# Four small edits around the attention and state-space stages of a two-layer encoder kernel

## The chip, the cores and the metric

The kernel runs on one core of one Trainium2 chip. The metric is the device time of one execution in microseconds (us).

## What is computed

The reference is a trunk of two layers on one sequence of 256 tokens of width 2048, all in float32. Cut to what matters here, a layer computes

```
h    = rms_norm(x)
proj = h @ w_in                    # cq 512 | ckv 256 + k_pe 64 | u 1024 | gates 2 x 2048
a    = mla(cq, ckv, k_pe)          # 16 heads: q, k of 128 + 64 (rope), v of 128
s    = s5(u)                       # 64 groups x 64 complex states, linear recurrence over time
m    = sigmoid(g_a) * a + sigmoid(g_b) * s
x    = x + rms_norm(m @ w_out)
x    = x + rms_norm(swiglu(rms_norm(x)) @ w_ffn_down)
```

Inside `mla`, a pair of heads at a time: `p = softmax(q k^T * scale)` with a block-causal mask, then `p @ v`. Inside `s5`: `bu = u @ B` (the input to each state), a recurrence along time, and `y = Re(C state) + D u`, then a gelu and a gated product with `w_glu`.

## The kernel before, in words

**Products.** Each float32 product is made of three products of float32r parts: a value is split into a high part (a copy that rounds) and a low part (value minus high part). Weights come from memory as tiles of 128x1024, one DMA on SP's queue each. ScalarE makes the high part `hi` (`Weights.high_to`, L179, its ACTIVATE at L187) and VectorE the low part `lo` (`split_to`, L191). `gemm` (L417) runs the three products at L448 to L450 for 16 row blocks of the weight; one `step` of it is six products on one half of the tokens. The products of an attention pair stand at L1387 to L1389 (q), L1414 to L1416 (k) and L1432 to L1434 (v).

**Order.** Instructions are emitted in an order written out by hand. `Background` (L74) is the planner. `later(d, fn)` puts a piece of work `d` steps ahead, `chain(d, fns)` puts several one step apart. `step(pe_ns)` (L118) adds one to the step count, emits what is due, and then emits pieces of the background generators as long as VectorE's planned time is less than `lead` ahead of TensorE's. Every VectorE instruction adds max(140, 75 + n/0.96) ns to VectorE's planned time, where n is the number of elements in a partition (`Counted`, L140, L150); ScalarE's instructions add nothing. All VectorE work goes through `Counted`, so it shows as L151 in the profile; ScalarE's goes through `act`, L268; a TensorE transpose is L494.

**S5.** `s5` (L915) is a background generator. It waits until its first state input is planned (`bu_due = bg.later(6, lambda: emit_bu(0))`, L1120), then runs 32 column tiles, each of which multiplies the tile's powers `E` with the state input `bu` (a tile `P` of 128x1024), adds, scans twice along time, multiplies again and adds to `xx`. `emit_bu` (L1069) is two TensorE products per tile, L1074; they read `us` and `bs`, stacked copies of u and of B that POOL fetches through memory (`load_stacks`, L1053, issues at L1063). After every four tiles `emit_y` (L1080) makes the output product, and a gelu of seven pieces writes `uz`. `prep_b` and `prep_c` transpose B and C into the bank `y`. The generator runs beside the input projections (stages u, ckv, cq, gates), the attention and the start of the product with `w_o`. `begin_glu` (L1466) empties the planner: it emits whatever of S5 is left, in the first product with `w_glu`, which reads `uz`, after six of its steps.

**Attention.** The loop over eight pairs (L1376) interleaves three pairs. At the top it makes the scores of the pair before (`scores`, L1311, products L1316 to L1319), and a step later come, one step each: the row maximum (VectorE), the exponentials (ScalarE), the reciprocal of the row sums (VectorE), the division (`norm`, L1339: four ScalarE ACTIVATEs, `p<-p,sts`). Below that stand q's rope part into the first half of `qp`, the product with v of two pairs before (`pv`, L1363; its output goes into `oT` in two parts, high on ScalarE two steps later and low on VectorE three steps later, shown as `H<-aux` and `H<-aux,H`), q's other two parts into `qn`, and the product that turns the rope part (L1401) into the second half of `qp`. A step later `rope` (L1219) reads it: `X<-X,rope`, `rtmp<-acc,rope`, `X<-X,rtmp`. Then k into `kk_ps`, the transposes of the divided exponentials (`trans_p`, L1347, shown as `aux<-cs,p`), and v into `v_ps`. ScalarE copies `qn`, `kk_ps` and `v_ps` out (`X<-acc` of 128x512).

`acc()` (L249) hands out one of three accumulator banks; a new tile waits until all readers of the bank's earlier tile are done. In the loop the four tiles `qp`, `qn`, `kk_ps`, `v_ps` of a pair share the three, so `v_ps` takes a bank of the same pair.

Of the kernel before, what the change touches and what calls it, by code (L numbers as in the profile page):

```python
# [13 lines left out]
AF = mybir.ActivationFunctionType  # L14
# [206 lines left out]
def trunk_kernel(ctx: ExitStack, tc: tile.TileContext, a: dict, out: bass.AP, cst: bass.AP,  # L221
# [27 lines left out]
    def acc():  # L249
        return T(pacc, [128, 512], "acc")  # L250
# [7 lines left out]
    def tsc(o, x, s1, op0, s2=None, op1=None):  # L258
        if op1 is None:
            V.tensor_scalar(out=o, in0=x, scalar1=s1, scalar2=None, op0=op0)  # L260
        else:
            V.tensor_scalar(out=o, in0=x, scalar1=s1, scalar2=s2, op0=op0, op1=op1)
# [4 lines left out]
    def act(o, x, f, **kw):  # L267
        ACT.activation(out=o, in_=x, func=f, **kw)  # L268
# [3 lines left out]
    def parts(hi, lo, src):  # L272
        return [lambda: act(hi, src, AF.Copy), lambda: tt(lo, src, hi.bitcast(F32), SUB)]
# [611 lines left out]
    for l in range(depth):  # L885
# [29 lines left out]
        def s5(l=l, gains=gains):  # L915
# [153 lines left out]
            def emit_bu(ct):  # L1069
                p, c = divmod(ct, 2)  # L1070
                bs, us = stacks[p]
                bu = T(ps5, [128, 2, S], "bu")
                for i in range(2):
                    PE.matmul(out=bu[:, i], lhsT=bs[:, c, 128 * i:128 * i + 128], rhs=us[:, c], start=True, stop=True)  # L1074
                bus[ct] = bu
                if c == 1:
                    used.append(p)
                    load_stacks()
# [38 lines left out]
            e_mirror(e)  # L1117
            while not stacks:
                yield
            bu_due = bg.later(6, lambda: emit_bu(0))  # L1120
            y_due = g_due = None
            xs = []
            yield
# [95 lines left out]
        def rope(dst, raw, rot):  # L1219
            tt(dst, raw, cosT, MUL)  # L1220
            tt(rtmp, rot, sinT, MUL)
            tt(dst, dst, rtmp, ADD)
# [88 lines left out]
        def scores(p, t):  # L1311
            sa, sb = aux(), aux()
            sa = sa.rearrange("p (h k) -> p h k", h=2)
            sb = sb[:, 0:256].rearrange("p (h k) -> p h k", h=2)
            for h_ in range(2):
                PE.matmul(out=sb[:, h_], lhsT=t["q"][:, h_, 0:128], rhs=t["k"][:, h_, 0:128], start=True, stop=False)  # L1316
                PE.matmul(out=sb[:, h_], lhsT=t["pe"][:, 0:128], rhs=kpeT[:, h_, 0:128], start=False, stop=True)
                PE.matmul(out=sa[:, h_], lhsT=t["q"][:, h_, 128:256], rhs=t["k"][:, h_], start=True, stop=False)
                PE.matmul(out=sa[:, h_], lhsT=t["pe"][:, 128:256], rhs=kpeT[:, h_], start=False, stop=True)  # L1319
            pr = T(ap, [128, 768], "p", bufs=2)  # L1320
            pb = pr[:, 0:256].rearrange("p (h k) -> p h k", h=2)
            pa = pr[:, 256:768].rearrange("p (h k) -> p h k", h=2)
            sts = T(vp, [128, 2, 4], "sts", bufs=2)

            def row_max():
                V.memset(ap=sb[0:64, :, 64:128], constant=NEG)
                V.memset(ap=sa[0:64, :, 192:256], constant=NEG)
                V.tensor_reduce(out=sts[:, 0, 0:2], in_=sb, axis=AX.X, op=ALU.max)
                V.tensor_reduce(out=sts[:, 0, 2:4], in_=sa, axis=AX.X, op=ALU.max)
                tsc(sts[:, 0], sts[:, 0], -SCALE, MUL)  # L1330

            def exps():
                for i, (s_, p_) in enumerate(((sb, pb), (sa, pa))):
                    for h_ in range(2):
                        j = 2 * i + h_
                        act(p_[:, h_], s_[:, h_], AF.Exp, scale=SCALE, bias=sts[:, 0, j:j + 1],
                            accum_out=sts[:, 1, j:j + 1])

            def norm():  # L1339
                for i, p_ in enumerate((pb, pa)):  # L1340
                    for h_ in range(2):
                        act(p_[:, h_], p_[:, h_], AF.Copy, scale=sts[:, 1, 2 * i + h_:2 * i + h_ + 1])

            bg.chain(1, [row_max, exps, lambda: V.reciprocal(out=sts[:, 1], in_=sts[:, 1]), norm])
            return pb, pa

        def trans_p(pp):  # L1347
# [15 lines left out]
        def pv(p, t, pT):  # L1363
            o = aux()
            for h_ in range(2):
                e = slice(128 * h_, 128 * h_ + 128)
                PE.matmul(out=o[:, 256 * h_:256 * h_ + 256], lhsT=t["v"][:, 0, e], rhs=pT[:, h_, 0:256],
                          start=True, stop=False)
                PE.matmul(out=o[:, 256 * h_ + 128:256 * h_ + 256], lhsT=t["v"][:, 1, e], rhs=pT[:, h_, 256:384],
                          start=False, stop=True)  # L1370
            bg.chain(2, parts(oT[:, 0, 2 * p:2 * p + 2], oT[:, 1, 2 * p:2 * p + 2],
                              o.rearrange("p (h t) -> p h t", h=2)))

        bg.lead = LEAD_ATT
# [1 line left out]
        for p in range(NPAIR):  # L1376
            t = par_tiles(p)
            if p >= 1:
                st_p[p - 1] = scores(p - 1, par_tiles(p - 1))
                bg.step(ATT * 2600)  # L1380
            base = W.pos
            qn, qp = None, acc()

            def proj(j, o):
                for k in range(4):
                    hi, lo = [t[:, k % 2, 128 * j:128 * j + 128] for t in W.get(base + k // 2, "q", base + 3)]
                    PE.matmul(out=o, lhsT=hi, rhs=cqT[:, 0, k], start=(k == 0), stop=False)  # L1387
                    PE.matmul(out=o, lhsT=lo, rhs=cqT[:, 0, k], start=False, stop=False)
                    PE.matmul(out=o, lhsT=hi, rhs=cqT[:, 1, k], start=False, stop=(k == 3))  # L1389

            proj(2, qp[:, 0:256])
            bg.step(ATT * 1300)
            bg.later(1, lambda t=t, qp=qp: act(t["raw"], qp[:, 0:256], AF.Copy))
            if p >= 2:
                pv(p - 2, par_tiles(p - 2), st_pT.pop(p - 2))
            bg.step(ATT * 1300)
            qn = acc()
            proj(0, qn[:, 0:256])
            bg.step(ATT * 1300)
            proj(1, qn[:, 256:512])  # L1400
            PE.matmul(out=qp[:, 256:512], lhsT=rperm, rhs=t["raw"], start=True, stop=True)  # L1401
            bg.later(1, lambda t=t, qp=qp: rope(t["pe"], t["raw"], qp[:, 256:512]))
            W.drop(base)
            W.drop(base + 1)
            bg.step(ATT * 1300)
            bg.later(1, lambda t=t, qn=qn: act(t["q"], qn.rearrange("p (h t) -> p h t", h=2), AF.Copy))
            base = W.pos
            hi, lo = W.get(base, "kv", base + 3)
            kk_ps = acc()
            for h_ in range(2):  # L1410
                o = kk_ps[:, 256 * h_:256 * h_ + 256]
                e = slice(256 * h_, 256 * h_ + 128)
                for k in range(2):
                    PE.matmul(out=o, lhsT=hi[:, k, e], rhs=ckvT[:, 0, k], start=(k == 0), stop=False)  # L1414
                    PE.matmul(out=o, lhsT=lo[:, k, e], rhs=ckvT[:, 0, k], start=False, stop=False)
                    PE.matmul(out=o, lhsT=hi[:, k, e], rhs=ckvT[:, 1, k], start=False, stop=(k == 1))  # L1416
            W.split_to(base + 1)
            bg.step(ATT * 1300)
            W.split_to(base + 2)
            bg.later(1, lambda t=t, kk_ps=kk_ps: act(t["k"], kk_ps.rearrange("p (h t) -> p h t", h=2), AF.Copy))  # L1420
            if p >= 1:
                st_pT[p - 1] = trans_p(st_p.pop(p - 1))
            bg.step(ATT * 650)
            v_ps = acc()
            hv = hi.rearrange("p k (h e) -> p k h e", h=2)[:, :, :, 128:256]
            lv = lo.rearrange("p k (h e) -> p k h e", h=2)[:, :, :, 128:256]
            for tb in range(NT):
                o = v_ps[:, 256 * tb:256 * tb + 256].rearrange("p (h e) -> p h e", h=2)
                for k in range(2):
                    xh = ckvT[:, 0, k, 128 * tb:128 * tb + 128]  # L1430
                    xl = ckvT[:, 1, k, 128 * tb:128 * tb + 128]
                    PE.matmul(out=o, lhsT=xh, rhs=hv[:, k], start=(k == 0), stop=False)  # L1432
                    PE.matmul(out=o, lhsT=xh, rhs=lv[:, k], start=False, stop=False)
                    PE.matmul(out=o, lhsT=xl, rhs=hv[:, k], start=False, stop=(k == 1))  # L1434
            W.drop(base)
            bg.later(1, lambda t=t, v_ps=v_ps: act(t["v"], v_ps.rearrange("p (b e) -> p b e", b=2), AF.Copy))
            bg.step(ATT * 1300)
# [188 lines left out]
```

## Time and profile before

| | us |
|---|---|
| median of three runs (2844.93 to 2863.11) | 2846.59 |
| the profiled execution | 2843.14 |
| its span, first to last instruction | 2841.4 |
| TensorE busy in the span | 2769.2 |
| VectorE busy | 1919.3 |
| ScalarE busy | 1459.3 |

The profiled execution is one run on the chip; what lies outside its span is 1.7 us. PE is TensorE, DVE is VectorE, ACT is ScalarE, POOL is GpSimd. In a row of a timeline the first two numbers are start and duration, and a bracket at the end is the idle time before the instruction and what ended it.

### The profile page before, as it was taken

The numbers are of one execution on the slowest core, as the hardware profiler recorded it, in microseconds if no ns is written. First come the engines' busy times: TensorE is split into PE (matmuls) and PEld (weight loads), VectorE is DVE, ScalarE is ACT, GpSimd is POOL, SyncE is SP. The second block draws the span as 40 slices with busy tenths as digits, with TensorE's granted clock in tenths as the row PEclk, the third lists the DMA queues.
The fourth block names the chain that finished last, engine by engine and source line by source line (L and its number), as shares of the span: only waits on it lengthen the run. The fifth ranks groups of instructions, "written<-read, shape, count | busy, mean of one in ns | idle before, by whom it ended". The sixth has DMA issues, their size and how long they took to land. (4 is left out here: it accounts for less than half of the span.)

```text
span 2841.4 us, 44618 instructions
## 1 busy us (share of the span) xinstructions
PE 2769.2 (97%) x16985; PEld 2451.1 (86%) x16985; DVE 1919.3 (68%) x2830; ACT 1459.3 (51%) x2477; POOL 224.5 (8%) x417
## 2 busy tenths in 40 slices
PE   8999889999999999999989999899999999999998
PEld 7888888887999999988868778888879999999887
DVE  7899988666666555544469999966665555555444
ACT  6666775444544444444457568844454444444433
POOL 1123130000000000000021322100010000000000
PEclk9999999999999999999999999999999999999999
DMA  7888456766666666666588985476666666667664
GB/s 231 245 254 239 119 140 215 241 219 211 201 206 201 205 193 189 206 197 197 179 250 227 249 231 144 137 231 220 222 215 196 198 193 197 186 192 239 198 198 143
DMA packets 331218, 579.41 MB, mean 204 GB/s; under 512 B 40768, under 2 KB 75004, under 8 KB 330620
## 3 DMA queue, kind: packets, MB, share of 16 engines
q1 hardware_dynamic: 292492, 526.33, 59.9%
q0 software_dynamic: 33728, 41.71, 6.0%
q10 hardware_dynamic: 4784, 8.53, 0.8%
q8 instruction: 133, 2.18, 0.3%
q14 instruction: 81, 0.66, 0.1%
HBM read 549.52 MB, written 26.95 MB: 203 GB/s over the span
## 5 line engine op out<-in xcount | busy, mean ns | idle before, releaser
L151 DVE TENSOR_TENSOR lo<-raw,hi 128x1024 fp32r<-128x1024 f32 (+3 forms) x992 | 1148.5, 1172 | 523.1 <-PE acc L449 225.5
L187 ACT ACTIVATE hi<-raw 128x1024 fp32r<-128x1024 f32 (+3 forms) x992 | 995.2, 1017 | 790.9 <-PE acc L450 244.6
L448 PE MATMUL acc<-hi,H 128*128 128x512 f32 (+1 forms) x1152 | 456.7, 396 | 6.3 <-DVE p L151 4.2
L450 PE MATMUL acc<-hi,H 128*128 128x512 f32 (+1 forms) x1152 | 447.5, 388 | 3.8 <-DVE H L151 3.6
L449 PE MATMUL acc<-lo,H 128*128 128x512 f32 (+1 forms) x1152 | 447.1, 388 | 1.0 <-DVE lo L151 0.8
L448 PE MATMUL acc<-hi,aT 128*128 128x512 f32 x704 | 274.4, 390 | 0.0
L449 PE MATMUL acc<-lo,aT 128*128 128x512 f32 x704 | 274.2, 389 | 0.0
L450 PE MATMUL acc<-hi,aT 128*128 128x512 f32 x704 | 274.2, 389 | 0.0
L474 PE MATMUL acc<-H,hi 128*128 128x256 f32 x960 | 265.9, 277 | 0.3
L476 PE MATMUL acc<-H,hi 128*128 128x256 f32 x960 | 265.4, 276 | 0.0
L475 PE MATMUL acc<-H,lo 128*128 128x256 f32 x960 | 265.4, 276 | 0.0
L476 PE MATMUL aux<-H,hi 128*128 128x256 f32 x960 | 265.4, 276 | 0.0
L474 PE MATMUL aux<-H,hi 128*128 128x256 f32 x960 | 265.3, 276 | 0.0
L475 PE MATMUL aux<-H,lo 128*128 128x256 f32 x960 | 265.3, 276 | 0.0
L448 PEld LDWEIGHTS acc<-hi,H 128*128 128x128 f32 x1152 | 217.8, 189 | 53.6 <-DVE p L151 7.2
L450 PEld LDWEIGHTS acc<-hi,H 128*128 128x128 f32 x1152 | 217.5, 189 | 52.0 <-DVE H L151 8.1
L449 PEld LDWEIGHTS acc<-lo,H 128*128 128x128 f32 x1152 | 217.9, 189 | 41.3 <-DVE lo L151 2.6
L474 PEld LDWEIGHTS acc<-H,hi 128*128 128x128 f32 x960 | 180.3, 188 | 0.8 <-DVE X L151 0.7
L475 PEld LDWEIGHTS acc<-H,lo 128*128 128x128 f32 x960 | 180.3, 188 | 0.1
L476 PEld LDWEIGHTS aux<-H,hi 128*128 128x128 f32 x960 | 180.3, 188 | 0.0
L476 PEld LDWEIGHTS acc<-H,hi 128*128 128x128 f32 x960 | 180.3, 188 | 0.0
L475 PEld LDWEIGHTS aux<-H,lo 128*128 128x128 f32 x960 | 180.2, 188 | 0.0
(231 smaller groups left out, 4884.6 us busy)
## 6 DMA issues: line engine op xcount, KB each, us to landing
raw<-in_w_in_dram SPq DMA_DIRECT2D x176, 512.0 KB, 4.8
raw<-in_w_ffn_gate_dram SPq DMA_DIRECT2D x176, 512.0 KB, 4.4
raw<-in_w_ffn_up_dram SPq DMA_DIRECT2D x176, 512.0 KB, 4.6
raw<-in_w_ffn_down_dram SPq DMA_DIRECT2D x176, 512.0 KB, 4.6
raw<-in_w_o_mla_dram SPq DMA_DIRECT2D x64, 512.0 KB, 4.6
raw<-in_w_glu_dram SPq DMA_DIRECT2D x64, 512.0 KB, 4.7
raw<-in_w_out_dram SPq DMA_DIRECT2D x64, 512.0 KB, 4.8
raw<-in_w_uq_dram SPq DMA_DIRECT2D x32, 384.0 KB, 3.9
```

The lines of the kernel that those rows point to most:

```text
L151: return f(**kw)
L187: self.nc.scalar.activation(out=dst(hv), in_=src(self.raw[n]), func=AF.Copy)
L448: PE.matmul(out=o, lhsT=xh, rhs=h[:, kk], start=(k == 0), stop=False)
L449: PE.matmul(out=o, lhsT=xh, rhs=lo[:, kk], start=False, stop=False)
L450: PE.matmul(out=o, lhsT=xl, rhs=h[:, kk], start=False, stop=(k == nk - 1))
L474: PE.matmul(out=o, lhsT=hw[:, kk, n], rhs=h[:, 0, k], start=(k == 0), stop=False)
L475: PE.matmul(out=o, lhsT=lw[:, kk, n], rhs=h[:, 0, k], start=False, stop=False)
L476: PE.matmul(out=o, lhsT=hw[:, kk, n], rhs=h[:, 1, k], start=False, stop=(k == nk - 1))
```

## The change

The division of the softmax moves from ScalarE to VectorE, as four `tensor_scalar` in the same step as the reciprocal, one step sooner than it was. The turned rope part goes into an accumulator bank of its own. The two parts of `pv`'s output come one step sooner each. The first state input is planned 10 (layer 0) or 15 (layer 1) steps ahead in place of 6.

```diff
-            bu_due = bg.later(6, lambda: emit_bu(0))
+            bu_due = bg.later(10 if l == 0 else 15, lambda: emit_bu(0))
...
             def norm():
                 for i, p_ in enumerate((pb, pa)):
                     for h_ in range(2):
-                        act(p_[:, h_], p_[:, h_], AF.Copy, scale=sts[:, 1, 2 * i + h_:2 * i + h_ + 1])
-
-            bg.chain(1, [row_max, exps, lambda: V.reciprocal(out=sts[:, 1], in_=sts[:, 1]), norm])
+                        tsc(p_[:, h_], p_[:, h_], sts[:, 1, 2 * i + h_:2 * i + h_ + 1], MUL)
+
+            bg.chain(1, [row_max, exps, lambda: (V.reciprocal(out=sts[:, 1], in_=sts[:, 1]), norm())])
...
-            bg.chain(2, parts(oT[:, 0, 2 * p:2 * p + 2], oT[:, 1, 2 * p:2 * p + 2],
+            bg.chain(1, parts(oT[:, 0, 2 * p:2 * p + 2], oT[:, 1, 2 * p:2 * p + 2],
                               o.rearrange("p (h t) -> p h t", h=2)))
...
-            PE.matmul(out=qp[:, 256:512], lhsT=rperm, rhs=t["raw"], start=True, stop=True)
-            bg.later(1, lambda t=t, qp=qp: rope(t["pe"], t["raw"], qp[:, 256:512]))
+            turned = acc()
+            PE.matmul(out=turned[:, 0:256], lhsT=rperm, rhs=t["raw"], start=True, stop=True)
+            bg.later(1, lambda t=t, turned=turned: rope(t["pe"], t["raw"], turned[:, 0:256]))
```

## Rows read from the trace of the kernel before

**Rows 1.** The page's first part: engine, busy us, share, instructions.

```profile
PE 2769.2 (97%) x16985; PEld 2451.1 (86%) x16985; DVE 1919.3 (68%) x2830; ACT 1459.3 (51%) x2477; POOL 224.5 (8%) x417
```

**Rows 2.** TensorE's waits in the whole span: us in total, times, longest.

```profile
PE acc L1432 <- DVE rtmp L151: 8.5, 9, 2.6
PE acc L1432 <- ACT X L268: 7.6, 3, 3.0
PE aux L1316 <- ACT X L268: 7.3, 8, 1.7
...
PE y L494 <- DVE bd L151: 3.6, 1, 3.6
```

**Rows 3.** Length, then busy PE, PEld, DVE, ACT, POOL, clock: seven pairs, both layers.

```profile
299.38:413.65 114.27, 98.55 (x701) 91.25 (x701) 99.37 (x197) 88.36 (x272) 23.88 (x44) 0.96 0.40 114
1724.27:1829.75 105.48, 93.91 (x695) 87.22 (x695) 98.77 (x196) 86.34 (x267) 22.82 (x42) 0.98 0.43 120
```

**Rows 4.** VectorE's waits in the same stretches, layer 0, then layer 1.

```profile
DVE E L151 <- ACT Et L268: 6.4, 6, 1.8
DVE P L151 <- ACT E L268: 4.0, 4, 2.3
...
DVE E L151 <- ACT Et L268: 3.3, 5, 1.1
...
DVE P L151 <- ACT E L268: 0.8, 1, 0.8
```

**Rows 5.** Timeline of one pair in layer 0: ScalarE, VectorE, TensorE.

```profile
372.73 1.50 ACT L268 ACTIVATE p<-p,sts 128x128 f32<-128x128 f32 x4 [1.64 <-DVE sts L151]
...
376.85 0.57 ACT L268 ACTIVATE X<-acc 128x512 f32<-128x512 f32 x1
...
378.00 0.42 DVE L151 TENSOR_TENSOR X<-X,rtmp 128x256 f32<-128x256 f32 x1
...
377.48 0.58 PE L1432 MATMUL acc<-hi,ckvT 128*128 128x256 f32 x1 [2.54 <-ACT X L268]
...
380.21 0.63 PE L1316 MATMUL aux<-X 128*128 128x128 f32 x2
```

**Rows 6.** Groups by form, whole span: count, then busy us, mean ns, idle before.

```profile
L268 ACT ACTIVATE p<-p,sts 128x256 f32<-128x256 f32 x32 | 14.4, 498 | 0.0
L268 ACT ACTIVATE p<-p,sts 128x128 f32<-128x128 f32 x32 | 11.2, 398 | 22.3 <-DVE sts L151 22.3
...
L151 DVE TENSOR_TENSOR_SCAN Z<-seeds,Z 128x256 f32<-128x256 f32 x128 | 81.4, 678 | 1.3
...
L151 DVE TENSOR_SCALAR X<-X 128x32 f32<-128x32 f32 x17 | 2.4, 179 | 0.1
...
L151 DVE TENSOR_SCALAR X<-X 128x256 f32<-128x256 f32 x4 | 1.2, 291 | 0.1
...
L151 DVE TENSOR_SCALAR B<-B,cs 128x256 f32<-128x256 f32 x1 | 0.4, 354 | 0.0
```

**Rows 7.** TensorE's timeline around the first state input of layer 1.

```profile
1489.75 0.77 PE L1074 MATMUL bu<-us,bs 128*128 128x256 f32 x2 [7.12 <-DMA us<-u_d]
1490.31 0.47 PE L448 MATMUL acc<-hi,H 128*128 128x320 f32 x1
...
1493.51 0.40 PE L1074 MATMUL bu<-us,bs 128*128 128x256 f32 x2
1493.74 0.31 PE L448 MATMUL acc<-hi,H 128*128 128x320 f32 x1
1493.89 0.31 PE L449 MATMUL acc<-lo,H 128*128 128x320 f32 x1
```

**Rows 8.** Instructions on `uz` from 380 to 620 us: duration, first and last start.

```profile
L448 PE MATMUL acc<-hi,uz x128: 388/390/486, 510.6 to 599.8; 128*128 128x512 f32 x128
...
L151 DVE SCALAR_TENSOR_TENSOR uz<-gelu,uz x3: 419/419/421, 426.9 to 490.8; 128x256 fp32r<-128x256 f32 x3
```

**Rows 9.** Groups by form, the seven pairs of layer 0: S5's first multiplication.

```profile
L151 DVE TENSOR_TENSOR P<-E,bu 128x1024 f32<-128x1024 f32 x10 | 12.2, 1216 | 4.2 <-ACT E L268 4.0
```

## The prediction

> **What bounds the kernel.** I read the page's first part, then TensorE's waits, then the stages of the largest ones. TensorE is busy 2769.2 of 2841.4 us [rows 1]: nearly everything is a stream of products whose number the change leaves alone, and only the 72.2 us in which TensorE stands still, and the time that it runs at the lower clock, can be won. Five of its waits bear on this change. Four are in the attention, 27.0 us together: v's products waiting for rope (8.5) and for ScalarE's copies (7.6), the scores waiting for ScalarE (7.3), a transpose of C waiting for VectorE (3.6) [rows 2]. The fifth is one state input that waits 7.12 us for a DMA [rows 7]. In the seven full pairs of layer 0, 114.27 us long, TensorE is busy 98.55 us, VectorE 99.37 and ScalarE 88.36; in layer 1 it is 93.91, 98.77 and 86.34 of 105.48 [rows 3]. The reader is to see that VectorE is the fullest engine there, and that it stands still largely because ScalarE does: of its 14.9 us idle in layer 0, 10.4 are waits for ScalarE's E and Et, and of 6.7 in layer 1, 4.1 [rows 4]. ScalarE in turn stands 22.3 us, over the 16 pairs, right ahead of the division, waiting for VectorE's reciprocal [rows 6]. So the two hold each other up, and TensorE waits for the later one.
>
> **First state input, layer 1.** The wait is 7.12 us and ends at 1489.75, so TensorE had come there at 1482.63. After it twelve products start 0.267 us apart (1490.31 to 1493.51) where they later start 0.147 apart (1493.74 to 1493.89): 1.4 us more [rows 7]. Fully removed this gives 8.5 us. Nine steps later: the input stands in the middle of the ckv product, with eight of its sixteen steps still to come, each six times 0.147, 0.88 us; the ninth step is of 512 columns where these are of 320, 1.6 times as long, 1.4 us. Together 8.5 us, so TensorE would come to the input at about 1491.1, where the copy of u has been there since 1489.7: margin 1.4 us. POOL issues this copy without waiting for TensorE, so I take it to land when it did. I take 8.5; bounds 6.5, if the copy lands some 3.4 us later, and 9.5, if a neighbouring wait goes too. What is late next: S5 starts nine steps later in the program, though only 1.4 us later on the clock.
>
> **First state input, layer 0.** No such wait stands in layer 0, so four steps more save nothing. S5 is put off by four steps of 512 columns, 5.6 us; what hides this is the room at its end, below. I take 0.
>
> **The division.** Per pair ScalarE loses two ACTIVATEs of 0.498 and two of 0.398 us, 1.79 us, and the wait ahead of them, 22.3 us over 16 pairs, 1.4 us [rows 6]: 3.2 us per pair. VectorE gains four `tensor_scalar` with a scalar per partition. The trace has one such at 256 elements, 354 ns, against 291 with a constant; at 32 elements it is 179 [rows 6]. For 128 elements I interpolate 228 and add the same 63: 291. Two of each: 1.29 us. Bounds: 0.9, if they overlap at their ends, and 1.8, ScalarE's own time. The planner counts 2 x 208 + 2 x 342 = 1,100 ns for them and hands out that much less S5. By its formula an S5 tile is planned at 4.53 us (two of 1,142, two of 608, two scans of 342, E parts 350); the scans alone last 678 each [rows 6], so a tile really costs at least 0.67 more, 15%, and what is shed is 1.26 us. VectorE's load per pair thus stays as it is: between -0.5 and +1.29 us (nothing shed).
>
> What is won is VectorE's idle time behind ScalarE, at most 10.4 + 4.1 = 14.5 us [rows 4]. The pair at 372 us shows it: v's products wait 2.54 us for the copy of q at 376.85, behind the division at 372.73, which stands 1.64 us for the reciprocal [rows 5]. With ScalarE 3.2 us earlier that wait goes. But rope's last add ends at 378.42, and the next scores, now at 380.21, need it: 1.79 us is all that this pair can win unless rope comes sooner too. VectorE is late next. Not every wait for Et stands behind the division, since S5's own multiplications alternate between the two engines as well. I take four fifths, 11.6 us. Bounds: a gain of all 27.0 us [rows 2] and the clock besides (0.96 of 114.27 and 0.98 of 105.48, at most 6.7 us [rows 3]), 33.7; and a loss of 14 x 1.29 = 18.1 us.
>
> By the Trainium skill ("SBUF — State Buffer", section "Who interferes with whom") a `tensor_scalar` from SBUF to SBUF can run in a mode that takes the port which GpSimd shares, and GpSimd then stands still until it ends. By that rule POOL's issues of S5's stacks would slip by up to the four operations in each pair. It speaks against the change, and no row of this trace shows the two side by side. In rows: POOL is busy 23.88 of 114.27 us [rows 3], so a slip of 1.29 us per pair finds room, and I take 0; as a rival it stands below.
>
> **Rope's own bank.** When v's products come, three tiles are still unread: before, `qp` (by rope), `qn` and `kk_ps`; after, the new one (by rope), `qn` and `kk_ps`, since `kk_ps` takes the bank of `qp`, whose only reader is long done. With three banks v waits for the first of the same three readers. I take 0; bounds 8.5 us won (v's wait for rope goes whole [rows 2]) and 3.0 lost (the turning product waits once for the copy of v of the pair before, as long as the longest wait of this kind in [rows 2]).
>
> **Output of `pv` a step sooner.** Same instructions, same engines. The high part stands ahead of the rest of ScalarE's queue as before, and the low part is further ahead of rope, which it already preceded. `pv` itself is covered by q's products after it; 0, bounds 0.6 us each way per layer, the length of such a part by the copy of 128x512 in [rows 5].
>
> **S5's end.** The shed work, eight pairs of 1.1 us planned, is 1.9 tiles of 4.53. In the attention ten tiles come in 114.27 us [rows 3, 9], 11.4 each: S5 of layer 0 ends 22 us later, and with the four steps 27.6, an upper bound, since after the attention less stands beside it on VectorE. Now it ends at 491.2 (490.8 + 0.42). The products with w_glu begin at 510.6; 128 of their first kind, two per step, take 89.2 us, so six steps later, at about 519, what is left of S5 is put out at once [rows 8]. Room: 27.8 us. It holds, barely. If it didn't, TensorE would wait for the last pieces of a gelu; I put half a tile's 11.4 us on that, 5.7. I take 0. In layer 1 the room is larger, since S5 starts there without the seeds to compute.
>
> **Sum.** 2843.1 - 8.5 - 11.6 = 2823.0 for the profiled execution, which is 3.5 us under the median of the three runs; I add nothing for that, since the range is far wider.
>
> **Rivals.**
> (1) The waits in the attention go whole and some of the clock with them: 2843.1 - 8.5 - 27.0 - 3 = 2804.6. For it: 14.9 of the 27.0 us end on ScalarE [rows 2], which is freed by 3.2 us per pair. Against it: VectorE's load of 98 to 99 us where TensorE's is 94 to 98 [rows 3].
> (2) Rope takes over: each wait for ScalarE that goes comes back as one for VectorE, and only the state input is won: 2834.6. For it: in [rows 5] rope's add starts 0.52 us after v's products.
> (3) Slower than before: the planner's shedding doesn't reach the pairs, because S5's pieces are handed out whole, and VectorE's load grows by the entire division, 18.1 us, ahead of rope, for which v and the scores wait: 2843.1 - 8.5 + 18.1 = 2852.7. It decides from the point where VectorE has no idle time left: 99.37 + 9.0 = 108.4 of 114.27 in layer 0 and 107.8 of 105.48 in layer 1 [rows 3], so it needs layer 1 full and layer 0 still waiting on ScalarE.
> (4) The port: every stack comes late by 1.29 us in each of 14 pairs, and TensorE stands in the state inputs as it does in [rows 7]: 2823.0 + 18.1 = 2841.1.
> (5) The state input's wait is only moved, because other transfers fill the time and the copy lands nine steps later too: 2843.1 - 11.6 = 2831.5.
>
> **How the numbers follow.** Forecast 0.50 (own range 2814 to 2831), (1) 0.20, (2) 0.17, (3) 0.07, (4) 0.02, (5) 0.04. The range 2804 to 2843 leaves out (3) and a tail of (1). One per cent, about what a measurement of this kernel can tell from no change, is 28.5 us below 2846.6: 2818.1. Faster by more than that: (1) and 0.08 of the forecast, 0.28. Slower by more than that, above 2875, needs (3) and an S5 that isn't done in time as well: 0.02. Same: 0.70.
>
> **What would show it.** No wait of L1074 on a DMA. No long wait of ScalarE for `sts` ahead of the transposes, and VectorE's waits for Et and E under half of the 14.5 us. `p<-p,sts` on VectorE at about 0.29 and 0.35 us. The stretches of seven pairs about 106 and 102 us long, what is left of L1432's waits mostly on rtmp. The last write of `uz` in layer 0 between 505 and 519 less what was won before it. Wrong would be: stretches as long as before with VectorE over 90% (rivals 2, 3), TensorE waiting at `uz`, or a wait of L1074 that is still there.

## The result, and the profile after

The changed kernel takes 2817.33 us (median of 15 runs) beside 2847.59 us for the kernel before (15 runs, same chip): ratio 0.9889, 95% interval 0.9858 to 0.9921. That is 0.8% to 1.4% faster; one per cent, which the prediction takes as about what can be told from no change, lies inside the interval. The profiled execution took 2813.43 us, its span is 2811.6, so between the two profiles 29.8 us of span went.

The page's first part after, against [rows 1]: VectorE has 64 instructions more and ScalarE 64 fewer, the division's 4 in each of 16 pairs.

```profile
PE 2764.7 (98%) x16985; PEld 2444.8 (87%) x16985; DVE 1933.0 (69%) x2894; ACT 1438.8 (51%) x2413; POOL 225.1 (8%) x417
```

TensorE's waits after, whole span (engine, tile, line, what it waited for; total us, times, longest), against [rows 2]. Lines from 1400 on have moved by one: L1433 is v's first product.

```profile
PE aux L1316 <- ACT X L268: 4.0, 3, 1.9
...
PE acc L1433 <- DVE rtmp L151: 2.2, 3, 0.9
...
PE acc L1433 <- ACT X L268: 1.6, 2, 1.2
...
PE bu L1074 <- DMA bs<-b_d: 0.7, 1, 0.7
```

v's waits fell from 8.5 and 7.6 to 2.2 and 1.6, the scores' from 7.3 to 4.0, and the transpose of C that waited 3.6 has no row near that size any more. Of 27.0 us, 7.8 are left.

The windows of the seven pairs after, layer 0 then layer 1 (columns as in [rows 3]):

```profile
299.07:397.75 98.68, 93.47 (x694) 85.99 (x693) 96.00 (x209) 74.87 (x226) 22.96 (x42) 1.00 0.45 129
1700.45:1798.70 98.25, 94.63 (x695) 87.26 (x693) 95.23 (x206) 74.63 (x225) 22.94 (x42) 0.98 0.46 129
```

The stretches became 15.6 and 7.2 us shorter, 22.8 together. Read each as VectorE's busy time plus its idle time. Busy went from 99.37 to 96.00 and from 98.77 to 95.23: 6.9 us less work. Idle went from 14.90 to 2.68 and from 6.71 to 3.02: 15.9 us. TensorE in layer 0 shows the same from its side: its busy time fell by 5.1 us with the granted clock going from 0.96 to 1.00, and its idle time by 10.5.

VectorE's waits in the same stretches after, against [rows 4]: two rows for layer 0, one for layer 1, and nothing is left of the waits for E.

```profile
DVE aux L151 <- PE aux L1319: 0.5, 1, 0.5
DVE E L151 <- ACT Et L268: 0.5, 1, 0.5
...
DVE aux L151 <- PE aux L1319: 1.3, 1, 1.3
```

The forms of the division after, whole span (count, then busy us, mean ns, idle before), against [rows 6]:

```profile
L151 DVE TENSOR_SCALAR p<-p,sts 128x256 f32<-128x256 f32 x32 | 9.9, 351 | 0.0
L151 DVE TENSOR_SCALAR p<-p,sts 128x128 f32<-128x128 f32 x32 | 7.8, 285 | 0.6
```

And S5's first multiplication in the seven pairs of layer 0, against [rows 9]: eight tiles where there were ten.

```profile
L151 DVE TENSOR_TENSOR P<-E,bu 128x1024 f32<-128x1024 f32 x8 | 9.7, 1217 | 0.6
```

The first state input of layer 1 after, against [rows 7]: TensorE waits 0.72 us there instead of 7.12, and for the other copy (B's).

```profile
1477.68 0.48 PE L1074 MATMUL bu<-us,bs 128*128 128x256 f32 x2 [0.72 <-DMA bs<-b_d]
```

The instructions on `uz` from 380 to 620 us after, against [rows 8] (duration, first and last start):

```profile
L448 PE MATMUL acc<-hi,uz x128: 388/389/499, 495.7 to 586.4; 128*128 128x512 f32 x128
...
L151 DVE SCALAR_TENSOR_TENSOR uz<-gelu,uz x4: 417/418/420, 379.8 to 500.7; 128x256 fp32r<-128x256 f32 x4
```

S5 of layer 0 now ends 5.4 us after the products with w_glu began (501.1 against 495.7); before it ended 19.4 us ahead of them. The shed work has moved to where [rows 8] had room for it. Beside the products with w_glu TensorE has one wait for VectorE's low parts of the weights that it hadn't before:

```profile
515.58 0.50 PE L449 MATMUL acc<-lo,uz 128*128 128x512 f32 x1 [0.42 <-DVE lo L151]
```

That S5's later end causes it isn't shown. It comes 14 us after that end, and shortly ahead of it VectorE stands 5.57 us for a transfer of `gate`, where before it stood 3.90 us; two of the kernels below, `no_rope_bank` and `pv_later`, in which S5 ends as late, have no such wait. VectorE's row after, then the same of before:

```profile
511.71 0.69 DVE L151 TENSOR_TENSOR sg<-sg,gate 128x512 f32<-128x512 f32 x1 [5.57 <-DMA gate<-sgb]
```

```profile
524.90 0.69 DVE L151 TENSOR_TENSOR sg<-sg,gate 128x512 f32<-128x512 f32 x1 [3.90 <-DMA gate<-sgb]
```

### The profile page after: what moved, and what is told of

Read it like the earlier page. It is cut to its first block, busy times and chain, and to the rows that moved or that the text cites. A ratio compares the mean times of both kernels' runs of the same rounds, so it can differ in the third digit from the quotient of the medians.

```text
span 2811.6 us, 44601 instructions
## 1 busy us (share of the span) xinstructions
PE 2764.7 (98%) x16985; PEld 2444.8 (87%) x16985; DVE 1933.0 (69%) x2894; ACT 1438.8 (51%) x2413; POOL 225.1 (8%) x417
## 4 chain that ended last, share of the span: by engine, by line
PE 82%; DVE 11%; DMA 2%; issue 2%; ACT 2%; SPq 0%; POOL 0%; ACTq 0%; DVEq 0%; POOLq 0%
PE acc L448 16%; PE acc L450 16%; PE acc L449 16%; PE acc L474 4%; PE aux L476 4%; PE aux L474 4%; PE aux L475 4%; PE acc L476 4%; PE acc L475 4%; DVE lo L151 3%; DVE P L151 2%; DVE Z L151 1%; PE bu L474 1%; PE y L476 1%; PE bu L476 1%
## 5 line engine op out<-in xcount | busy, mean ns | idle before, releaser
L476 PEld LDWEIGHTS aux<-H,hi 128*128 128x128 f32 x960 | 180.2, 188 | 0.0
L474 PEld LDWEIGHTS aux<-H,hi 128*128 128x128 f32 x960 | 180.2, 188 | 0.0
```

The lines of the kernel that those rows point to most:

```text
L474: PE.matmul(out=o, lhsT=hw[:, kk, n], rhs=h[:, 0, k], start=(k == 0), stop=False)
L476: PE.matmul(out=o, lhsT=hw[:, kk, n], rhs=h[:, 1, k], start=False, stop=(k == nk - 1))
```

## The experiments

Each is compared with the kernel before on its own chip; the stretches are the seven pairs of each layer, as in [rows 3].

### The division alone, and its two halves

`div_only` is the kernel before with the division's edit and nothing else.

```diff
-                        act(p_[:, h_], p_[:, h_], AF.Copy, scale=sts[:, 1, 2 * i + h_:2 * i + h_ + 1])
+                        tsc(p_[:, h_], p_[:, h_], sts[:, 1, 2 * i + h_:2 * i + h_ + 1], MUL)
...
-            bg.chain(1, [row_max, exps, lambda: V.reciprocal(out=sts[:, 1], in_=sts[:, 1]), norm])
+            bg.chain(1, [row_max, exps, lambda: (V.reciprocal(out=sts[:, 1], in_=sts[:, 1]), norm())])
```

> The kernel before with the division on VectorE alone. My theory (the division leaves ScalarE, and the planner hands out about two S5 tiles less per seven pairs): the seven pairs of layer 0 take about 99 us and of layer 1 about 98, as with the whole change, the first state input of layer 1 still waits about 7 us, and the time is about 22 us under the kernel before. Rival (the time came from rope's bank or the earlier split of pv's output): stretches above 108 and 102, time within 8 us of the kernel before.

`div_unplanned` is the same, but the division goes to VectorE past the planner, which is not told of it, so that it hands out as much of S5 as before:

```diff
-                        act(p_[:, h_], p_[:, h_], AF.Copy, scale=sts[:, 1, 2 * i + h_:2 * i + h_ + 1])
+                        nc.vector.tensor_scalar(out=p_[:, h_], in0=p_[:, h_], scalar1=sts[:, 1, 2 * i + h_:2 * i + h_ + 1],
+                                                scalar2=None, op0=MUL)
```

> The kernel before with the division on VectorE, but not charged to VectorE's planned time, so that the planner hands out as much S5 in the attention as before. Theory A (both the freed ScalarE and the shed S5 are needed): VectorE is busy 105 us or more per stretch, the stretches are about 110 and 108 us long, the time is within 6 us of the kernel before. Theory B (the shedding alone counts): VectorE's load grows by 15.6 us over both stretches and the time with it, about 15 us over the kernel before. Theory C (freeing ScalarE alone counts): stretches 99 and 98, about 22 us under it.

`plan_only` is the opposite: the division stays on ScalarE, and the planner is charged for it as if it stood on VectorE:

```diff
                     for h_ in range(2):
+                        bg.dve += 75 + (128 + 128 * i) / 0.96
                         act(p_[:, h_], p_[:, h_], AF.Copy, scale=sts[:, 1, 2 * i + h_:2 * i + h_ + 1])
```

> The kernel before, the division still on ScalarE, but VectorE's planned time charged with the 1.1 us per pair that the division would take there, so that the planner hands out less S5. Theory A: ScalarE's waits for the reciprocal stay, stretches about 108 and 102 us, some 9 us under the kernel before. Theory B (the shedding alone counts): stretches 99 and 98, about 22 us under it. Theory C (freeing ScalarE alone counts): stretches 114 and 105, no change.

Measured: `div_only` 2821.65 us, ratio 0.9914 (0.9897 to 0.9931); `div_unplanned` 2843.86 us, 0.9985 (0.9972 to 0.9998); `plan_only` 2831.63 us, 0.9948 (0.9932 to 0.9965). In us, by the ratios, that is 24.5, 4.3 (0.6 to 8.0) and 14.8 under the kernel before. The windows of `div_unplanned`, near what Theory A said:

```profile
301.13:410.60 109.47, 97.40 (x701) 89.83 (x701) 104.85 (x223) 80.58 (x247) 23.75 (x44) 0.97 0.42 118
1722.01:1828.47 106.46, 94.18 (x694) 86.93 (x694) 103.69 (x220) 77.76 (x239) 23.07 (x42) 0.98 0.43 119
```

those of `plan_only`, which no theory met whole (layer 1 near A's 102 us, layer 0 6 us under A's 108, and the time between A's 9 us and B's 22):

```profile
299.30:401.05 101.75, 93.04 (x694) 85.83 (x695) 92.12 (x184) 84.44 (x260) 22.86 (x42) 1.00 0.44 125
1712.71:1815.55 102.84, 92.92 (x692) 85.64 (x693) 91.07 (x183) 83.70 (x256) 22.82 (x42) 1.00 0.44 124
```

and those of `div_only`, which came out as expected:

```profile
299.48:397.64 98.16, 93.26 (x695) 86.10 (x695) 96.53 (x209) 75.58 (x232) 23.02 (x42) 1.00 0.46 129
1709.58:1807.35 97.77, 92.21 (x692) 85.84 (x693) 96.09 (x209) 74.55 (x228) 22.87 (x42) 1.00 0.47 130
```

Split as above into VectorE's work and idle time, both layers added (idle is the length less the busy time):

| kernel | both stretches | VectorE's work | VectorE idle |
|---|---|---|---|
| before | 219.8 | 198.1 | 21.6 |
| planner charged only (`plan_only`) | 204.6 | 183.2 | 21.4 |
| division moved, not charged (`div_unplanned`) | 215.9 | 208.5 | 7.4 |
| both (`div_only`) | 195.9 | 192.6 | 3.3 |
| the changed kernel | 196.9 | 191.2 | 5.7 |

The table tells the two halves apart. Charging the planner takes 15.0 us of work out of the pairs and leaves the idle time where it was. Moving the division takes 14.2 us of idle time out and puts 10.4 us of work in. Both figures of work are net: the windows of `plan_only` hold two more low parts of weights than those of before, 2.4 us, and those of `div_unplanned` three rope and three S5 instructions fewer, some 2.7 us. The first alone is worth 15.2 us, the second alone 3.8, both together 23.8, which is 4.8 more than the two added up. These rest on one profile each, and the same attention took between 112.4 and 116.8 us in layer 0 in three profiles (next section), so the 3.8 and the 4.8 aren't clear of that; the whole times above give the same order. So most of what the move brings in the attention would have come from handing out less of S5 there, without moving anything. Rival (3), in which the shedding doesn't reach the pairs, is what `div_unplanned` builds: even that isn't slower than before. The idle time removed (14.2) outweighs the work added (10.4).

The price of the division is smaller than its rows say. VectorE's instructions start before the one ahead has ended by the rows; the changed kernel's timeline of one pair shows it (start, duration):

```profile
365.38 0.17 DVE L151 RECIPROCAL sts<-sts 128x4 f32<-128x4 f32 x1
365.59 1.01 DVE L151 TENSOR_SCALAR p<-p,sts 128x128 f32<-128x128 f32 x4
366.51 0.68 DVE L151 TENSOR_TENSOR H<-aux,H 128x512 fp32r<-128x512 f32 x1
...
368.49 0.42 DVE L151 TENSOR_TENSOR X<-X,rtmp 128x256 f32<-128x256 f32 x1
...
368.50 0.36 PE L1433 MATMUL acc<-hi,ckvT 128*128 128x256 f32 x1
...
370.44 0.39 PE L1316 MATMUL aux<-X 128*128 128x128 f32 x2
```

The four take 0.92 us from the first start to the next instruction's start, where two of each mean sum to 1.27. Of the seven pairs of this stretch six give 0.92 or 0.93 and one 1.02, and `div_unplanned` agrees: 10.4 us and the 2.7 that left its windows, over 14 pairs, are 0.94. The same rows show what became of the pair in [rows 5]: here v's product stands without a wait, rope's add starts beside it, and the next scores start 1.94 us after that v product, where before they started 2.73 us after one.

### The later state input alone

`bu_only` is the kernel before with the first line of the change.

```diff
-            bu_due = bg.later(6, lambda: emit_bu(0))
+            bu_due = bg.later(10 if l == 0 else 15, lambda: emit_bu(0))
```

> The kernel before with the later first state input alone. My theory: L1074 waits under 1 us for a DMA, the stretches of seven pairs stay at about 114 and 105 us, the time is about 8.5 us under the kernel before. Rival (S5 starting later also lightens the attention): stretches shorter by 3 us or more.

Measured: 2841.5 us, ratio 0.998 (0.9957 to 1.0003). The wait went, 0.26 us of it are left, but the seven pairs of layer 1 grew from 105.48 to 113.24 us and gave 7.8 us back in this profile. The medians are 4.7 us apart, and the interval, from 12.2 us faster to 0.9 slower, holds the expected 8.5 as well as nothing. The window of layer 1, and TensorE's largest wait over the whole span (8.5 in [rows 2]):

```profile
1715.32:1828.56 113.24, 99.20 (x713) 90.31 (x711) 99.98 (x196) 86.65 (x267) 22.81 (x42) 0.95 0.39 113
```

```profile
PE acc L1432 <- DVE rtmp L151: 19.8, 11, 3.6
```

So the expectation of an unchanged attention fell. Two further runs asked whether a later start makes the attention longer as such, or whether its pieces only fall otherwise between the pairs' own instructions. `bu1_11` and `bu1_22` are the kernel before with 11 and 22 steps in layer 1 and 6 in layer 0:

```diff
-            bu_due = bg.later(6, lambda: emit_bu(0))
+            bu_due = bg.later(6 if l == 0 else 22, lambda: emit_bu(0))
```

> The kernel before with the first state input of layer 1 eleven steps ahead and nothing else. Theory A (the 8.5 us that the later input wins are given back because S5 then cuts its pieces otherwise against the pairs, and no order stands in how): five steps later end most of the wait (five times 0.88 us, so 2 to 4 us of the 7.1 are left or none), and the seven pairs of layer 1 take anything between 105 and 114 us. Theory B (the later S5 starts, the more of it falls into the attention): 109 to 110 us, between the 105.5 of the kernel before and the 113.2 of fifteen steps. Seven pairs of layer 0 as before, 114 us.

> As the run with eleven steps, with twenty-two. Theory A: no wait of the state input, the seven pairs of layer 1 between 105 and 114 us, not longer than with fifteen steps by any rule. Theory B: longer than with fifteen steps, 117 us or more, and a total 4 us or more above the run with fifteen steps, 2845 us.

Measured: 2870.07 us, ratio 1.0031 (0.9998 to 1.0064), and 2854.91 us, 0.9976 (0.994 to 1.0013); some 17 us of each of these medians, and of that of the kernel before, lie in another stage (last section), so the windows tell more. `bu1_11` still waits 4.1 us for its state input, a little over the 2 to 4 expected; `bu1_22` doesn't wait. Both layers of `bu1_11`:

```profile
298.67:415.48 116.81, 101.59 (x700) 93.72 (x701) 99.18 (x197) 88.26 (x272) 23.99 (x44) 0.93 0.39 111
1740.56:1857.53 116.97, 100.40 (x713) 91.94 (x713) 99.36 (x196) 87.45 (x269) 22.87 (x42) 0.94 0.38 109
```

and of `bu1_22`:

```profile
299.42:411.84 112.42, 97.17 (x700) 89.61 (x701) 99.15 (x197) 88.00 (x272) 24.43 (x45) 0.97 0.41 115
1734.20:1841.35 107.15, 97.35 (x712) 89.39 (x713) 97.79 (x194) 86.04 (x267) 28.50 (x53) 0.97 0.46 125
```

With 6, 11, 15 and 22 steps the pairs of layer 1 take 105.5, 117.0, 113.2 and 107.2 us. No order stands in that, so the theory that a later start lengthens the attention falls. The other was right that there is none, though its own upper end of 114 was too low. Part of the scatter isn't the edit's at all: layer 0, where these two kernels are the kernel before, took 116.8 and 112.4 us, where 114 was expected. In the kernels that have the division on VectorE and charge it as the change does, the same stretch of layer 1 lies between 96.5 and 98.5 us, whether the input comes after 6 steps (97.8 in `div_only`) or 15. What lengthens one stretch and not another, piece by piece, was not followed and stays open.

With the division in place, the later input keeps its gain: `div_only` still waits 7.4 us there, and its span is 2819.9 us against the changed kernel's 2811.6. The two stretches are 1.0 us shorter in `div_only`, so 9.3 us lie elsewhere.

```profile
PE bu L1074 <- DMA bs<-b_d: 7.4, 1, 7.4
```

### The small edits, each taken back

`no_rope_bank` is the changed kernel with the turned queries in the second half of `qp` again, `pv_later` with the output of `pv` a step later again, `bu0_sooner` with 6 steps in layer 0.

```diff
-            turned = acc()
-            PE.matmul(out=turned[:, 0:256], lhsT=rperm, rhs=t["raw"], start=True, stop=True)
-            bg.later(1, lambda t=t, turned=turned: rope(t["pe"], t["raw"], turned[:, 0:256]))
+            PE.matmul(out=qp[:, 256:512], lhsT=rperm, rhs=t["raw"], start=True, stop=True)
+            bg.later(1, lambda t=t, qp=qp: rope(t["pe"], t["raw"], qp[:, 256:512]))
```

> The changed kernel with the turned rope part back in the second half of qp. My theory (three readers for three banks, whichever way): v's products wait as long as with the change within 3 us, the stretches of seven pairs stay at about 99 and 98 us, the time stays within 4 us of the changed kernel. Rival (the own bank frees v from rope): v's waits for rtmp come back to 6 us or more and the time is 5 us or more above it.

```diff
-            bg.chain(1, parts(oT[:, 0, 2 * p:2 * p + 2], oT[:, 1, 2 * p:2 * p + 2],
+            bg.chain(2, parts(oT[:, 0, 2 * p:2 * p + 2], oT[:, 1, 2 * p:2 * p + 2],
```

> The changed kernel with pv's output split two and three steps later again. My theory: within 4 us of the changed kernel, stretches about 99 and 98 us. Rival (the low part right ahead of rope makes rope late): waits for rtmp grow by 3 us or more and the time by as much.

```diff
-            bu_due = bg.later(10 if l == 0 else 15, lambda: emit_bu(0))
+            bu_due = bg.later(6 if l == 0 else 15, lambda: emit_bu(0))
```

> The changed kernel with the first state input of layer 0 six steps ahead again. My theory: no wait of L1074 in layer 0, S5 of layer 0 writes its last part of uz about 5 us earlier (at about 496), the time is within 3 us of the changed kernel. Rival (the later start in layer 0 saves something by itself): 4 us or more above it.

Measured: 2813.57 us, ratio 0.9898 (0.9857 to 0.9939); 2814.34 us, 0.9888 (0.9848 to 0.9928); 2814.31 us, 0.9895 (0.9862 to 0.9929). None can be told from the changed kernel's 0.9889, as each theory said. The stretches agree: 98.7 and 98.5 us, 97.6 and 96.5, 98.2 and 97.0. Without rope's bank, TensorE's waits for the bank that v takes are all but the changed kernel's. These are its rows:

```profile
PE acc L1432 <- DVE rtmp L151: 2.2, 3, 1.0
...
PE acc L1432 <- ACT X L268: 1.6, 2, 1.2
```

In `bu0_sooner` the last `uz` starts at 494.6 us instead of 500.7, so the four steps put S5 off by 6.1 us and cost nothing that these runs can tell.

### Shedding more

Since charging the planner was the larger half, `lighter` charges it beyond the division's own time: 300 ns more per pair in layer 0, 700 in layer 1, with 6 steps in layer 0.

```diff
             def norm():
+                bg.dve += 300 if l == 0 else 700
                 for i, p_ in enumerate((pb, pa)):
```

> The changed kernel with the first state input of layer 0 six steps ahead and VectorE's planned time charged with 0.3 (layer 0) or 0.7 us (layer 1) more in each pair, so that still less S5 stands in the attention. If VectorE is what bounds the pairs now: its load falls by about 2.5 and 6 us per stretch, the stretches come to about 97 and 95 us, TensorE's load, and the time to about 3 to 5 us under the changed kernel. If TensorE already bounds them: no change; and if S5 of layer 0 then ends too late, TensorE waits at uz and the time is above it.

Measured: 2817.42 us, ratio 0.9899 (0.9868 to 0.993). Its windows:

```profile
299.39:398.87 99.48, 94.09 (x692) 87.42 (x693) 93.98 (x205) 74.13 (x223) 22.97 (x42) 0.98 0.45 128
1703.21:1795.19 91.98, 90.70 (x692) 85.40 (x691) 90.65 (x200) 72.67 (x217) 22.52 (x41) 1.00 0.46 133
```

In layer 1 the stretch lost another 6.3 us against the changed kernel, more than expected; TensorE, with 90.70 busy of 91.98, is now what sets it. Layer 0 won nothing though VectorE had 2.0 us less to do. The whole time can't be told from the changed kernel's, so a better version isn't shown; the last section says what speaks for one.

## Why the prediction was right, and where it wasn't

The forecast of 2823.0 is 5.7 us above the median and 9.6 above the profiled execution, and the range holds both. The sum was made for the profiled execution, though, and its 2813.4 lies just outside the forecast's own 2814 to 2831 and a little nearer to rival (1), 2804.6, than to the forecast: the wide range held more than the sum did. The sign and the places were right, the size of one term wasn't. The likeliest class, within one per cent, can't be told from faster: the interval goes to either side of it.

**The step that failed: the attention's 11.6 us.** Measured are 22.8. Two parts of it went wrong. "I take four fifths" of "VectorE's idle time behind ScalarE, at most 10.4 + 4.1 = 14.5 us" was too careful: of the waits for E and Et 0.5 us are left, so 14.0 of 14.5 went, and VectorE's idle time as a whole fell by 15.9. The one pair read in a timeline seemed to say that rope holds the rest back "unless rope comes sooner too". It did, but only with both halves of the edit: v's waits for rope, 8.5 us before, are these in `plan_only` and `div_unplanned`, and `div_only` has no such row (there the scores wait 2.5 us for VectorE instead).

```profile
PE acc L1433 <- DVE rtmp L151: 8.3, 10, 2.1
```

```profile
PE acc L1433 <- DVE rtmp L151: 5.7, 4, 2.7
```

And "VectorE's load per pair thus stays as it is" set a second gain to zero. The forecast weighed 1.29 us added against 1.26 shed. The shedding was sized well: `plan_only` gives 15.0 and the 2.4 us of weight parts that entered its windows, over 14 pairs, 1.24. The price was sized too high: 0.94 by `div_unplanned`. The net of these, -0.3, lies inside the stated -0.5 to +1.29; the windows of the changed kernel give 6.9 / 14, -0.49, at its low end, and what makes the rest was not followed. The prediction had a lower price in hand, 0.9 "if they overlap at their ends", and chose the sum of the row means. The timeline shows 0.92, so the ends do overlap.

**The state input's 8.5 us** was right in size and place: 7.12 us of wait became 0.72, and the span outside the two stretches shrank by 29.8 - 22.8 = 7.0. Outside the stretches `bu_only` (layer 0's is 113.7 us there) is 7.6 us shorter than the kernel before, and the changed kernel 9.3 shorter than `div_only`, so three pairs of profiles, with the 7.0, agree within 2.3 us. The margin of 1.4 us wasn't there: TensorE waited 0.72, for the copy of B where the working had looked at that of u. What the prediction didn't see is that the next stage can give the gain back: by the windows 11.5 us with 11 steps, 7.8 with 15 and 1.7 with 22, without the division. It was added as if the stages were independent; with the division in place that held. That it held because VectorE's idle time had gone from the pairs is a reading that no run tests.

**The terms set to zero** held: rope's bank, `pv`'s output, layer 0's later input, each within what a run can tell. **S5's end** held as narrowly as "It holds, barely" said: the room was put at 27.8 us, the use at 27.6 at most; S5's end moved by 24.8 us against the first product with w_glu (from 19.4 ahead to 5.4 behind), and at most one wait of 0.42 us came of it. "VectorE is late next" held in part: of v's waits 2.2 us are on rtmp and 1.6 on ScalarE, but with the scores' 4.0 most of the 7.8 us left end on ScalarE. ScalarE in turn no longer waits for a reciprocal, but longer for VectorE's row maxima ahead of its exponentials. The rows of layer 0 and of layer 1 after, 14.6 us together, where before the exponentials waited 1.3 and 3.6 us for them:

```profile
ACT p L268 <- DVE sts L151: 5.7, 4, 2.9
```

```profile
ACT p L268 <- DVE sts L151: 8.9, 4, 4.3
```

Two signs of "What would show it" missed: the stretches, given as about 106 and 102 us, and the wait of L1074, which is small but there.

**The rivals.** (1), 27.0 and 3 us won in the attention, lies 7.2 us beyond the 22.8 measured, the forecast 11.2 us short of it: of the two (1) was the nearer on this term. Its mechanism came true in part: 19.2 of the 27.0 us of waits went, and layer 0's clock went from 0.96 to 1.00. (2) falls, since what went in ScalarE's rows didn't come back in VectorE's. (3) falls by `div_unplanned`, which has its condition and isn't slower. (5) falls with the wait of 0.72. (4) would have shown as stacks that come late: no wait on a stack longer than 0.72 us stands at TensorE after, so it costs nothing here. The stacks' issues themselves can't tell more: none of the 16 of `us` in the stretch of layer 0 stands beside a division. Another of POOL's issues does, at 365.76, beside the four divisions at 365.59 shown above, and takes as long as one that has none beside it:

```profile
313.13 0.72 POOL L1049 DMA_DIRECT2D b_d<-bd  x1 [25.00 <-DVE E L151]
...
365.76 0.72 POOL L1049 DMA_DIRECT2D b_d<-bd  x1 [38.52 <-DVE sts L151]
```

By the rule of the Trainium skill ("SBUF — State Buffer", section "Who interferes with whom") GpSimd stands still while a `tensor_scalar` holds the port that the two share, if it runs in a mode that takes it. These rows don't show it, and one issue doesn't disprove it.

## What to carry to other kernels

When an operation moves to an engine that a planner fills with background work, ask first what the planner will hand out less: here that alone was worth 15.2 us in the attention, the move itself 3.8, by one profile each. Take the price of back-to-back VectorE instructions from start to start in a timeline, not from the sum of their mean durations. A wait removed in one stage counts only after the next stage's slack has been looked at, because the stage that inherits the shift may give it back.

## What was unexpected of the hardware

Single executions of one kernel fall into groups some 17 us apart. The traces show where: the gate and up products of one layer, a stage in which TensorE never stands still, run at one of two paces. These are the windows of 50 us at 800 us, of the kernel before and then of `bu1_22`, whose instructions there are the same:

```profile
800.00:850.00 50.00, 50.00 (x443) 50.00 (x443) 34.50 (x85) 22.14 (x24) 1.08 (x2) 1.00 0.65 203
```

```profile
800.00:850.00 50.00, 50.00 (x427) 50.00 (x426) 32.70 (x80) 22.05 (x23) 1.08 (x2) 1.00 0.63 200
```

TensorE is busy throughout and the granted clock reads 1.00 in both, but 427 products pass instead of 443: 0.117 us from start to start, evenly, instead of 0.113. `bu1_22` had it in layer 0 alone, the profiled execution of `no_rope_bank` in layer 1 alone (2831.31 us where the other runs of that kernel took about 2813.5). Its cause stays open. For the comparison of two profiles it means: look at the count of products in a stage that is full before a difference of 17 us is put down to an edit.

It bears on `lighter` too, whose profile has 427 in the same stage of layer 1. Three of its six executions took 2824.4 to 2827.4 us, the other three 2807.9 to 2810.4, less than any of the changed kernel's fifteen (2813.4 and more); on its own chip seven of the ten of `bu0_sooner`, which is `lighter` without the further charge, took 2809.2 to 2816.9. That points to the 3 to 5 us expected of `lighter`, but three executions don't show it.
